# A macaron transformer block on one core: attention taken head pair by head pair over both token halves, output projections moved between the last pairs, and new rules in the planner that orders the instructions

## Chip, cores and metric

The kernel runs on one core of a Trainium2 chip. The metric is the device time of one execution in microseconds (us), lower is better. Engines are named as in the profile: PE (TensorE matmul), PEld (its weight loads), DVE (VectorE), ACT (ScalarE), POOL (GpSimd) and SP (SyncE, which here only issues DMAs).

## What is computed

One layer of a bidirectional encoder over 512 tokens of width 1024, all in float32:

```python
h = h + 0.5 * rms_norm(swiglu(rms_norm(h, ffn1_pre_g), w_gu, w_down), ffn1_post_g)
z = rms_norm(h, mix_pre_g) @ w_in
q_na, k_na, v_na, c_q, c_kv, k_rope = jnp.split(z, split_at, axis=-1)
o_na = neighbourhood_attention(q_na, k_na, v_na, na_rpb)          # 8 heads of 64, 8 x 16 window
o_mla = latent_attention(c_q, c_kv, k_rope, ...)                  # 8 heads, latent q 256, kv 128
mixed = jnp.concatenate([rms_norm(o_na, na_out_norm_g),
                         rms_norm(o_mla, mla_out_norm_g)], axis=-1) @ w_out
h = h + rms_norm(mixed, mix_post_g)
h = h + 0.5 * rms_norm(swiglu(rms_norm(h, ffn2_pre_g), w_gu, w_down), ffn2_post_g)
```

The hidden width of both FFNs is 2816.

## The kernel before, in words

Tokens are held in four tiles of 128 (n = 0 to 3). A float32 product is made of three matmuls on operands split into a high and a low part (`mm3`): high by high, high by low, low by high. Every operand that PE reads in this way must first be cast (ACT, the high part) and subtracted (DVE or POOL, the low part); `split` does both, `load_w` fetches a weight block by DMA and splits it.

The stages in order: FFN1 (`ffn`: first chunks as plain products, the rest in a Winograd form with fewer multiplications), the mixer, FFN2. The mixer runs neighbourhood attention in four head pairs (`na_pair`), the latent compression, the latent attention (`mla_pair(j, hf)`, L1019: head pair j for the token half hf; half 1 holds tokens 2 and 3), and the output projection in two parts. `w_out_a(n, wo)` (L1062) projects the neighbourhood heads of token tile n, two groups of 12 matmuls of 512 columns, one for each half of the output columns. `w_out_b(n, b0, hr)` (L1072) projects the latent heads (24 matmuls), and then runs the token's norms on DVE, ACT and POOL: add, root mean square (`row_rms`: ACT squares with a running sum, DVE scales, POOL raises to the power -1/2), gain, residual, a second norm (FFN2's), and `put_xT`, which transposes the result on PE and splits it for FFN2. In an `mla_pair` a 512-column score tile goes from PE to DVE (row minimum), ACT (exponential), PE (four transposes), ACT and DVE (split), and PE again (product with the values, 256 columns). `put_o` (L773) scales and splits the head outputs and keeps squares for the group's norm, which `o_rstd` (L799) finishes with matmuls of 2 columns.

In the mixer's main sequence (L1089 to L1108) the four pairs of half 1 come first, each with a whole `w_out_a` behind it, then the four pairs of half 0, then `w_out_b` for tokens 2, 3, 0, 1:

```python
for j in range(4):
    mla_pair(j, 1)
    w_out_a((2, 3, 0, 1)[j], wo)
rB = o_rstd(1, (2, 3))
...
for j in range(4):
    mla_pair(j, 0)
```

That order in the code is only the starting point. The class `Plan` (L44) records every instruction with its dependencies (`runs`, `touch`, `add`) and a cost by a small model, places all of them forwards and backwards six times (`place`, `issue`), each time with priorities from the pass before, and at last issues them in the order of the best forward pass. On the chip each engine executes its instructions in that order; an engine whose next instruction waits does nothing behind it. All engine instructions are issued in one line of `issue`, L220 in the profile, so they are told apart by engine, operation and shape.

Of the kernel before, what the change touches and what calls it, by code (L numbers as in the profile page):

```python
# [18 lines left out]
P = 128  # L19
# [24 lines left out]
class Plan:  # L44
# [3 lines left out]
    TAIL = {"ACT": 95, "DVE": 75, "POOL": 60, "PE": 176}  # L48
# [16 lines left out]
    def runs(x):  # L65
# [20 lines left out]
        if kind == "psum":  # L86
            runs = sorted({(a // 512 * 512, (b + 511) // 512 * 512) for a, b in runs})
# [21 lines left out]
    def add(self, eng, op, a, k):  # L109
# [22 lines left out]
        elif eng == "PE":  # L132
            busy = max(109, (cols + 32) / 2.4)
# [15 lines left out]
    def place(self, prio, back):  # L149
# [12 lines left out]
        while done < n:  # L162
            t, e = min((max(free[e], 0.0 if ready[e] else soon[e][0][0]), e) for e in free if ready[e] or soon[e])
            ahead = 0 if e == "PE" or e == "SP" else 250
            while soon[e] and soon[e][0][0] <= t + ahead:
                s, p, i = heappop(soon[e])
                heappush(ready[e], (p, i))
            p, i = heappop(ready[e])
# [5 lines left out]
            if e == "PE" and not back:  # L174
                if s > idle + 1900:
                    warm = s + 3400
                if s < warm:
                    busy *= 2 if busy > 110 else 1.2
                idle = s + busy
            free[e] = s + busy  # L180
            if xfer:
                if back:
                    x = max(s + 500, dma)
                    dma = x + xfer
                    end = dma + 1300 + 330
                else:
                    x = max(s + busy + 1300, dma)
                    dma = x + xfer
                    end = dma + 500
            else:  # L190
                end = s + busy + tail
# [37 lines left out]
def hybrid_block(ctx, tc, A, out):  # L229
# [47 lines left out]
    sqr = cut(512, 1, 2688)  # L277
# [492 lines left out]
    sqs = [h[0][:, 512:], tokt.rearrange("p n c -> p (n c)")]  # L770
    last_sq = [None, None]

    def put_o(j, ps, c0=0):  # L773
# [7 lines left out]
        acc = sqs[g][:, :w]  # L781
        g = j // 4
# [10 lines left out]
        sq = sqr.get()[:, :w]  # L793
        square(sq)
        last_sq[g] = sq
# [3 lines left out]
    def o_rstd(g, ns):  # L799
# [3 lines left out]
        for i, v in enumerate((sqs[g], last_sq[g])):  # L803
            for n in range(len(ns)):
                PE.matmul(b[:, 2 * n : 2 * n + 2], v[:, n * P : (n + 1) * P], ones, start=i + n == 0,
                          stop=i == 1, skip_group_check=True)
# [212 lines left out]
    def mla_pair(j, hf):  # L1019
# [33 lines left out]
        by_column(l, 4, scr[:, 2944:], [r[:, :P], r[:, P:]])  # L1053
# [8 lines left out]
    def w_out_a(n, wo):  # L1062
        t = slice(n * P, (n + 1) * P)
        for hf in range(2):
            c = slice(hf * 512, hf * 512 + 512)
            ps = bank(nb())
            for j in range(4):
                oh, ol = oT[j]
                mm3(ps, (oh[:, t], ol[:, t]), (wo[j][0][:, c], wo[j][1][:, c]), j == 0, j == 3)
            ACT.activation(h[n][:, c], ps, AF.Copy, scale=rA[:, n : n + 1])  # L1070

    def w_out_b(n, b0, hr):  # L1072
# [4 lines left out]
        for j in range(4):  # L1077
            oh, ol = oT[4 + j]
            for hf in range(2):
                c = slice(hf * 512, hf * 512 + 512)  # L1080
                mm3(ps[:, c], (oh[:, t], ol[:, t]), (wo[j][0][:, c], wo[j][1][:, c]), j == 0, j == 3)
        DVE.scalar_tensor_tensor(mx, ps, rB[:, n : n + 1], mx, ALU.mult, ALU.add)
        r = row_rms(mx, ps, 1.0 / 32, EPS, bst)
# [3 lines left out]
        put_xT(n, norm(n, gn, hr, ps, bst), (b0, b0 + 1), mx)  # L1087
# [14 lines left out]
    for j in range(4):  # L1102
# [97 lines left out]
```

## Time and profile before

| what | value |
| --- | --- |
| median of 3 runs | 966.41 us (966.3 to 966.68) |
| the profiled execution | 969.88 us, span 968.1 us |
| mean granted PE clock of the span | 0.991 |
| PE, PEld busy | 948.5 us (98%), 851.8 us (88%) |
| DVE, ACT, POOL busy | 692.8 us (72%), 464.5 us (48%), 302.0 us (31%) |
| DMA | 130.11 MB, mean 134 GB/s |

The profiled execution is 3.47 us above the median. Busy time counts an instruction from start to end; a PE instruction that runs at a lower clock is busy for longer. A row of the view of busy time by stretch has the stretch and its length, then busy time and number of instructions of PE, PEld, DVE, ACT and POOL, then PE's granted clock as a share of full speed (1.00 is 2.4 GHz, 0.50 is 1.2 GHz), the DMA engines' busy share and GB/s. A row of a group by form ends with busy time and mean ns of one instruction, then idle time before them and what ended it. A row in time begins with start and length; the bracket at its end is the idle time of the engine before that row and what ended it. Some matmul records can be missing from a trace.

### The profile page before, as it was taken

The page shows a single profiled execution, that of the slowest core. Times are in us where ns is not written, and L with a number is a line of the kernel's source. Part 1 is how long each engine was busy: PE and PEld are TensorE (multiplying, and loading weights), DVE is VectorE, ACT ScalarE, POOL GpSimd, SP SyncE. Part 2 cuts the span into 40 slices and gives each one's busy share as a digit, 9 for nine tenths or more (in the row PEclk, how much of TensorE's full clock was granted, in tenths as well). Part 3 has the DMA queues.
Part 4 walks back from the last instruction along what each step waited for, and adds up shares of the span by engine and source line. Part 5 has one row for each costly group of instructions (what it writes and reads, how often), then busy time and mean ns, then how long its engine had stood idle before and what let it go on. Part 6 is the DMA issues. An engine that isn't in the chain of part 4 may idle for free. (4 is left out here: it accounts for less than half of the span.)

```text
span 968.1 us, 15209 instructions
## 1 busy us (share of the span) xinstructions
PE 948.5 (98%) x5878; PEld 851.8 (88%) x5878; DVE 692.8 (72%) x963; ACT 464.5 (48%) x801; POOL 302.0 (31%) x240
## 2 busy tenths in 40 slices
PE   9999999999999999999999989899999999999997
PEld 7788999999888888888988878799999999988885
DVE  4896999998522385567686587998999999742224
ACT  5553454444421362677567765764444444441211
POOL 0002767650000013222351422227777574000000
PEclk9999999999999999999999999999999999999999
DMA  9644334359743446122370112454433436753312
GB/s 288 205 156 131 128 132 145 117 155 306 225 113 96 140 159 131 62 75 45 109 165 1 66 44 88 152 183 136 151 120 110 152 127 217 250 170 109 87 44 87
DMA packets 60905, 130.11 MB, mean 134 GB/s; under 512 B 21920, under 2 KB 22816, under 8 KB 60832
## 3 DMA queue, kind: packets, MB, share of 16 engines
q1 hardware_dynamic: 59248, 126.25, 41.6%
q0 software_dynamic: 1008, 1.84, 1.1%
q10 hardware_dynamic: 576, 1.05, 0.3%
q8 instruction: 46, 0.75, 0.3%
q14 instruction: 27, 0.22, 0.1%
HBM read 109.45 MB, written 17.83 MB: 131 GB/s over the span
## 5 line engine op out<-in xcount | busy, mean ns | idle before, releaser
L220 PE MATMUL psum<-memr 128*128 128x256 f32 (+2 forms) x5520 | 921.9, 327 | 7.7 <-ACT memr L220 3.1
L220 PEld LDWEIGHTS psum<-memr 128*128 128x128 f32 x5520 | 809.6, 191 | 94.8 <-DVE memr L220 7.4
L220 DVE TENSOR_TENSOR memr<-m,memr 128x512 fp32r<-128x512 f32 (+3 forms) x310 | 353.7, 1168 | 144.1 <-ACT memr L220 143.9
L220 POOL TENSOR_TENSOR m<-m 128x512 f32<-128x512 f32 (+3 forms) x193 | 264.5, 1385 | 476.0 <-DVE m L220 368.3
L220 ACT CAST memr<-m 128x512 fp32r<-128x512 f32 (+3 forms) x318 | 259.9, 843 | 297.9 <-PE psum L220 213.5
L220 DVE TENSOR_TENSOR m<-psum,m 128x512 f32<-128x512 f32 (+3 forms) x205 | 119.9, 589 | 36.0 <-ACT m L220 21.7
L220 DVE TENSOR_TENSOR memr<-psum,memr 128x512 fp32r<-128x512 f32 (+3 forms) x116 | 68.0, 603 | 30.7 <-ACT memr L220 29.6
L220 ACT CAST memr<-psum 128x512 fp32r<-128x512 f32 (+3 forms) x124 | 62.4, 524 | 41.6 <-PE psum L220 31.8
L220 DVE TENSOR_TENSOR m<-m 128x512 f32<-128x512 f32 (+2 forms) x73 | 72.1, 999 | 6.9 <-ACT m L220 6.0
L220 PE MATMUL psum<-m 128*128 128x128 f32 (+1 forms) x358 | 58.2, 289 | 4.6 <-DVE m L220 2.8
L220 ACT ACTIVATE m<-m 128x512 f32<-128x512 f32 (+3 forms) x78 | 43.9, 564 | 33.1 <-DVE m L220 33.0
L220 PEld LDWEIGHTS psum<-m 128*128 128x128 f32 x358 | 46.6, 162 | 13.8 <-DVE m L220 3.3
L220 ACT COPY m<-psum 128x256 f32<-128x256 f32 (+2 forms) x63 | 26.1, 414 | 46.0 <-PE psum L220 33.9
L220 DVE SCALAR_TENSOR_TENSOR m<-m 128x512 f32<-128x512 f32 (+1 forms) x36 | 33.5, 966 | 4.8 <-POOL m L220 4.3
L220 ACT ACTIVATE m<-psum,m 128x512 f32<-128x512 f32 x40 | 27.4, 688 | 10.9 <-DVE m L220 10.1
L220 POOL MEMSET memr<- 128x256 f32 x8 | 2.5, 312 | 95.9 <-PE psum L220 95.9
L220 ACT ACTIVATE m<-psum 128x512 f32<-128x512 f32 (+2 forms) x27 | 14.0, 519 | 35.8 <-PE psum L220 35.8
L220 ACT ACTIVATE psum<-m 128x1024 f32<-128x1024 f32 x16 | 16.5, 1029 | 16.7 <-DVE m L220 12.1
L220 DVE TENSOR_REDUCE m<-psum 128x1 f32<-128x512 f32 x32 | 21.2, 684 | 1.0 <-PE psum L220 0.7
L220 DVE TENSOR_SCALAR m<-m 128x1 f32<-128x1 f32 (+1 forms) x36 | 6.2, 179 | 21.7 <-ACT m L220 12.2
L220 POOL TENSOR_TENSOR memr<-m,memr 128x1024 fp32r<-128x1024 f32 x8 | 19.3, 2426 | 5.1 <-ACT memr L220 5.1
L220 POOL CAST memr<-memr 64x512 fp32r<-64x512 f32 x8 | 5.8, 730 | 40.6 <-DVE memr L220 40.4
(23 smaller groups left out, 104.8 us busy)
## 6 DMA issues: line engine op xcount, KB each, us to landing
m<-in_ffn_w_gu SPq DMA_DIRECT2D x86, 512.0 KB
m<-in_ffn_w_down SPq DMA_DIRECT2D x44, 512.0 KB
gd<-m SPq DMA_DIRECT2D x44, 256.0 KB
m<-gd SPq DMA_DIRECT2D x44, 256.0 KB
m<-in_x SPq DMA_DIRECT2D x8, 512.0 KB
m<-in_w_qk SPq DMA_DIRECT2D x8, 512.0 KB
h<-m SPq DMA_DIRECT2D x8, 512.0 KB
m<-in_w_out SPq DMA_DIRECT2D x8, 512.0 KB
```

Of the source, the lines that this page charges most:

```text
L220: r = getattr(self.engines[eng], op)(*a, **k)
```

## The change

Two things are changed: the rules by which the planner orders instructions, and the order in which the mixer is written.

Planner: psum dependencies are kept for a whole bank rather than for each half of the partitions; a float32 matmul costs twice; the time from the end of an instruction to the start of one that waits for it on another engine is a number per engine (LAG) in place of 40 ns; SP is held back when DMAs pile up; only longer matmuls keep the modelled clock up; and an engine takes the best ready instruction, or one that becomes ready before that would end if it has a higher priority.

Mixer: the pairs come as (0,1), (0,0), (1,1), (1,0), (2,1), (3,1), each with one or two half projections `w_out_a(n, hf)` of 12 matmuls; then (2,0), `w_out_b(2)`, (3,0), `w_out_b(3)`, `w_out_b(0)`, `w_out_b(1)`. The second set of projection weights gets slots of its own (`w_b`) and is loaded between the pairs. Some scratch tiles move; the squares of `row_rms` in `w_out_b` go to SBUF instead of psum. The number of instructions of each kind stays the same.

```diff
+    ahead, margin = 250, 0
+    TAIL = {"ACT": 95, "DVE": 75, "POOL": 45, "PE": 176}
+    LAG = {"ACT": 60, "DVE": 50, "POOL": 85, "PE": 120, "SP": 60}
...
-            runs = sorted({(a // 512 * 512, (b + 511) // 512 * 512) for a, b in runs})
+            return [((kind, 0), sorted({(a // 512 * 512, (b + 511) // 512 * 512) for a, b in runs}))]
...
-            busy = max(109, (cols + 32) / 2.4)
+            busy = max(109, (cols + 32) / 2.4) * (1 + (op == "matmul" and a[1].dtype == F32))
...
-            ahead = 0 if e == "PE" or e == "SP" else 250
-            while soon[e] and soon[e][0][0] <= t + ahead:
+            while soon[e] and soon[e][0][0] <= t:
...
+            p, i = ready[e][0]
+            if e != "PE" and e != "SP" and soon[e]:
+                c = min(((q, s, j) for s, q, j in soon[e] if s < t + min(ops[i][5], self.ahead)), default=(p, 0, i))
+                if c[0] < p - self.margin:
...
+                    free[e] = max(free[e], dma - 4000) if e == "SP" else free[e]
...
-                est[j] = max(est[j], s + busy if ops[j][0] == e and not xfer else end + 40)
+                same = ops[j][0] == e and not xfer
+                est[j] = max(est[j], s + busy if same else end + (self.LAG[e] + ops[j][6] if back else self.LAG[ops[j][0]]))
...
-        r = row_rms(mx, ps, 1.0 / 32, EPS, bst)
+        sq = reg(Q_AT[6] + 256, 1)
...
+        r = row_rms(mx.rearrange("p (a b c) -> p a b c", a=2, b=2), sq, 1.0 / 32, EPS, bst)
...
-    wo = [load_w(A["w_out"][j], eng=POOL) for j in range(4)]
-    for j in range(4):
-        mla_pair(j, 1)
-        w_out_a((2, 3, 0, 1)[j], wo)
+    wa = [load_w(A["w_out"][j], eng=POOL) for j in range(4)]
+    gp, gn = load_g("mix_post_g"), load_g("ffn2_pre_g")
+    wb = [w_b(0)]
+    parts = [(n, hf) for n in (2, 3, 0, 1) for hf in range(2)]
+    for i, (j, hf) in enumerate(((0, 1), (0, 0), (1, 1), (1, 0), (2, 1), (3, 1))):
+        mla_pair(j, hf)
+        for _ in range((2, 1, 1, 1, 2, 1)[i]):
+            w_out_a(*parts.pop(0))
+        if i == 1:
+            wb.append(w_b(1))
+        if i == 3:
+            wb += [w_b(2), w_b(3)]
     rB = o_rstd(1, (2, 3))
     xb[1] = 26624
-    gp, gn = load_g("mix_post_g"), load_g("ffn2_pre_g")
-    wo = [load_w(A["w_out"][4 + j], eng=POOL) for j in range(4)]
-    for j in range(4):
-        mla_pair(j, 0)
-    for n in (2, 3):
-        w_out_b(n, 5, raws.get())
+    mla_pair(2, 0)
+    w_out_b(2, 5, raws.get())
+    mla_pair(3, 0)
+    w_out_b(3, 5, raws.get())
     o_rstd(1, (0, 1))
-    for n in (0, 1):
-        w_out_b(n, 2 * n, tmps.get())
+    w_out_b(0, 5, tmps.get())
+    w_out_b(1, 0, tmps.get())
```

How the order of the instructions changes, at the three places of which the prediction speaks. The issuing line is L220 before and L233 after. Names: `in_x` are rows of the input, `in_ffn_w_gu` blocks of FFN1's gate and up weights, `m_63` and `memr` the two big SBUF tensors, `gd_68` a DRAM scratch.

SP at the start of the program, before:

```order
L220 DMA m_63<-in_ffn_w_gu 128x1024
L220 DMA m_63<-in_x 128x1x1024 x4
L220 DMA m_63<-in_ident 128x128
L220 DMA m_63<-in_g_o 128x8
L220 DMA m_63<-in_tokt 128x256
L220 DMA m_63<-in_ffn_w_gu 128x1024 x6
L220 DMA gd_68<-m_63 128x512
```

and in the changed kernel:

```order
L233 DMA m_63<-in_ffn_w_gu 128x1024 x2
L233 DMA m_63<-in_x 128x1x1024 x2
L233 DMA m_63<-in_ident 128x128
L233 DMA m_63<-in_x 128x1x1024 x2
L233 DMA m_63<-in_ffn_w_gu 128x1024 x3
L233 DMA m_63<-in_g_o 128x8
L233 DMA m_63<-in_tokt 128x256
L233 DMA m_63<-in_ffn_w_gu 128x1024 x3
```

The second weight block moved ahead of the four rows of the input, and the third to fifth ahead of two small tables.

PE at the start, before (the 128-column matmuls behind the 72 are the first that need rows of the input):

```order
L220 MATMUL psum<-m_63 128x128 x11
L220 MATMUL psum<-memr 128x512 x72
L220 MATMUL psum<-m_63 128x128 x4
L220 MATMUL psum<-memr 128x512 x264
L220 MATMUL psum<-memr 128x256 x1260
```

and in the changed kernel:

```order
L233 MATMUL psum<-m_63 128x128 x11
L233 MATMUL psum<-memr 128x512 x67
L233 MATMUL psum<-m_63 128x128
L233 MATMUL psum<-memr 128x512 x7
L233 MATMUL psum<-m_63 128x128
L233 MATMUL psum<-memr 128x512 x8
L233 MATMUL psum<-m_63 128x128
L233 MATMUL psum<-memr 128x512 x7
L233 MATMUL psum<-m_63 128x128
L233 MATMUL psum<-memr 128x512 x247
L233 MATMUL psum<-memr 128x256 x1260
```

The four products that stood together behind 72 wide matmuls now stand singly, the first behind 67, with 7 or 8 wide ones between them.

PE in the last attention pairs (512 columns: scores and projections; 128: transposes; 256: products with the values), before:

```order
L220 MATMUL psum<-memr 128x256
L220 MATMUL psum<-m_63 128x128 x2
L220 MATMUL psum<-memr 128x256 x7
L220 MATMUL psum<-m_63 128x128 x6
L220 MATMUL psum<-memr 128x512 x6
L220 MATMUL psum<-memr 128x256 x8
L220 MATMUL psum<-m_63 128x128 x4
L220 MATMUL psum<-memr 128x512 x2
L220 MATMUL psum<-m_63 128x128 x4
L220 MATMUL psum<-memr 128x512 x2
L220 MATMUL psum<-m_63 128x128 x4
L220 MATMUL psum<-memr 128x512 x2
```

and in the changed kernel:

```order
L233 MATMUL psum<-memr 128x512 x33
L233 MATMUL psum<-m_63 128x128 x8
L233 MATMUL psum<-memr 128x512 x4
L233 MATMUL psum<-m_63 128x128 x2
L233 MATMUL psum<-memr 128x512 x7
L233 MATMUL psum<-m_63 128x128 x8
L233 MATMUL psum<-memr 128x512 x5
L233 MATMUL psum<-memr 128x256
L233 MATMUL psum<-memr 128x512 x2
L233 MATMUL psum<-m_63 128x128 x4
L233 MATMUL psum<-memr 128x512
L233 MATMUL psum<-memr 128x256 x7
```

The runs of 33, 7 and 5 now hold projections of `w_out_b` among the scores, and the group of 8 at the second row is a token's transposes for FFN2; before, neither stood at this point.

PE at the end of the mixer, before (the three groups of 128 are transposes of the tokens for FFN2, the 256-column matmuls already FFN2's):

```order
L220 MATMUL psum<-memr 128x512 x40
L220 MATMUL psum<-m_63 128x128 x8
L220 MATMUL psum<-memr 128x512 x8
L220 MATMUL psum<-memr 128x256 x28
L220 MATMUL psum<-m_63 128x128 x8
L220 MATMUL psum<-memr 128x256 x10
L220 MATMUL psum<-m_63 128x128 x8
L220 MATMUL psum<-memr 128x256 x154
```

and in the changed kernel:

```order
L233 MATMUL psum<-memr 128x512 x6
L233 MATMUL psum<-memr 128x256 x68
L233 MATMUL psum<-m_63 128x128 x8
L233 MATMUL psum<-memr 128x256 x26
L233 MATMUL psum<-m_63 128x128 x8
L233 MATMUL psum<-memr 128x256 x96
L233 MATMUL psum<-memr 128x512 x48
```

The groups of FFN2 matmuls ahead of the last two groups of transposes grew from 28 and 10 to 68 and 26; the first group of transposes of before now stands earlier, between the attention pairs.

## Rows read from the trace of the kernel before

**Rows 1.** The page: busy time by engine, share of the span.
```profile
PE 948.5 (98%) x5878; PEld 851.8 (88%) x5878; DVE 692.8 (72%) x963; ACT 464.5 (48%) x801; POOL 302.0 (31%) x240
```

**Rows 2.** Busy time by stretch: FFN1; attention pairs with projections between.
```profile
100.00:200.00 100.00, 100.00 (x836) 100.00 (x835) 98.62 (x102) 46.54 (x71) 69.26 (x41) 1.00 0.42 138
485.00:568.00 83.00, 83.00 (x462) 69.73 (x462) 58.92 (x104) 58.58 (x121) 29.13 (x29) 1.00 0.29 74
```

**Rows 3.** PE in time: a run of 512 columns, one of 128.
```profile
484.74 20.51 PE L220 MATMUL psum<-memr 128*128 128x512 f32 x89 [0.21 <-ACT memr L220]
476.61 2.28 PE L220 MATMUL psum<-m 128*128 128x128 f32 x20
```

**Rows 4.** Stretches where PE loses time; small matmuls 476.7 to 484.7.
```profile
23.24:29.96 6.72, 4.79 (x16) 3.24 (x15) 3.98 (x7) 4.12 (x6) 0.55 (x1) 0.75 0.56 184
399.00:476.00 77.00, 76.10 (x456) 67.45 (x457) 52.10 (x171) 54.48 (x149) 21.78 (x34) 1.00 0.24 57
476.61:485.20 8.59, 8.29 (x45) 6.76 (x44) 6.23 (x15) 5.86 (x13) 5.12 (x5) 0.80 0.74 245
568.20:584.00 15.80, 12.54 (x65) 10.33 (x64) 13.19 (x24) 10.55 (x26) 3.72 (x5) 0.78 0.08 33
606.20:620.00 13.80, 9.66 (x65) 8.03 (x64) 12.43 (x15) 8.53 (x16) 4.77 (x4) 1.00 0.54 184
L220 PE MATMUL psum<-m 128*128 128x128 f32 x16 | 3.1, 331 | 0.1
L220 PE MATMUL psum<-m 128*128 128x2 f32 x16 | 1.8, 246 | 0.0
```

**Rows 5.** Busy time by stretch: the three at half clock.
```profile
26.50:29.90 3.40, 3.35 (x7) 2.24 (x8) 3.40 (x5) 2.88 (x4) 0.00 (x0) 0.50 0.39 82
480.46:483.87 3.41, 3.41 (x14) 2.80 (x12) 1.98 (x4) 3.02 (x5) 2.73 (x2) 0.50 0.91 334
576.00:582.90 6.90, 5.97 (x22) 5.18 (x23) 4.80 (x8) 4.04 (x10) 1.52 (x3) 0.51 0.00 0
```

**Rows 6.** Opening in time: PE restart, first and last square, second weight cast.
```profile
26.44 5.74 PE L220 MATMUL psum<-memr 128*128 128x512 f32 x16 [1.44 <-ACT memr L220]
15.42 1.03 ACT L220 ACTIVATE psum<-m 128x1024 f32<-128x1024 f32 x1 [1.26 <-DMA m<-in_x]
22.18 1.03 ACT L220 ACTIVATE psum<-m 128x1024 f32<-128x1024 f32 x1 [1.11 <-DMA m<-in_x]
25.34 1.04 ACT L220 CAST memr<-m 128x1024 fp32r<-128x1024 f32 x1 [2.02 <-DMA m<-in_ffn_w_gu]
```

**Rows 7.** PE by form, 568.2 to 584, and one of its waits in time.
```profile
L220 PE MATMUL psum<-m 128*128 128x128 f32 x28 | 6.0, 345 | 1.7 <-ACT m L220 1.7
L220 PE MATMUL psum<-memr 128*128 128x512 f32 x13 | 5.6, 542 | 0.0
L220 PE MATMUL psum<-memr 128*128 128x256 f32 x24 | 4.5, 316 | 1.6 <-DVE memr L220 0.9 <-ACT memr L220 0.4 <-DVE m L220 0.3
574.47 1.09 PE L220 MATMUL psum<-memr 128*128 128x256 f32 x7 [0.87 <-DVE memr L220]
```

**Rows 8.** PE and DVE by form, 606.2 to 620; POOL's powers in time.
```profile
L220 PE MATMUL psum<-memr 128*128 128x256 f32 x38 | 5.7, 293 | 2.8 <-DVE m L220 1.4 <-ACT m L220 0.7 <-DVE memr L220 0.7
L220 PE MATMUL psum<-m 128*128 128x128 f32 x19 | 2.6, 277 | 1.3 <-DVE m L220 1.3
L220 PE MATMUL psum<-memr 128*128 128x512 f32 x8 | 2.1, 403 | 0.0
L220 DVE SCALAR_TENSOR_TENSOR m<-m 128x1024 f32<-128x1024 f32 x4 | 5.1, 1284 | 1.3 <-POOL m L220 1.3
L220 DVE TENSOR_TENSOR m<-m 128x1024 f32<-128x1024 f32 x2 | 2.4, 1218 | 0.0
603.48 0.54 POOL L220 TENSOR_TENSOR m<-m 128x1 f32<-128x1 f32 x1 [3.75 <-DVE m L220]
605.49 1.45 POOL L220 TENSOR_TENSOR m<-m 128x1 f32<-128x1 f32 x1 [1.46 <-DVE m L220]
```

More of the change, by code (lines that the diff above doesn't have):

```diff
@@ L3 @@
 from contextlib import ExitStack
-from heapq import heappop, heappush
+from heapq import heapify, heappop, heappush
 import numpy as np
@@ L44 @@
 class Plan:
-    TAIL = {"ACT": 95, "DVE": 75, "POOL": 60, "PE": 176}
+    ahead, margin = 250, 0
+    TAIL = {"ACT": 95, "DVE": 75, "POOL": 45, "PE": 176}
+    LAG = {"ACT": 60, "DVE": 50, "POOL": 85, "PE": 120, "SP": 60}
     def __init__(self, tc):
@@ L178, in place @@
                     busy *= 2 if busy > 110 else 1.2
-                idle = s + busy
+                if busy > 115:
+                    idle = s + busy
             free[e] = s + busy
@@ L185, in place @@
                     end = dma + 1300 + 330
+                    free[e] = max(free[e], dma - 4000)
                 else:
@@ L189, in place @@
                     end = dma + 500
+                    free[e] = max(free[e], dma - 4000) if e == "SP" else free[e]
             else:
-                end = s + busy + tail
+                end = s + busy + (0 if back else tail)
             start[i] = s if not back else -(end if xfer else s + busy)
@@ L276, in hybrid_block @@
     tmps = cut(1024, 3)
-    sqr = cut(512, 1, 2688)
+    sqr = scr[:, 2688:3200]
     bst = Ring([new(8) for _ in range(8)])
@@ L769, in hybrid_block @@
     Q_AT = (7168, 5120, 18432, 19456, 20480, 12288, 13312, 25600)
-    sqs = [h[0][:, 512:], tokt.rearrange("p n c -> p (n c)")]
-    last_sq = [None, None]
+    W_AT = ((4096, 4608, 6144, 6656), (7168, 7680, 21504, 22016), (18432, 18944, 22528, 23040), (23552, 24064, 15872, 17920))
+    sqs = [h[0][:, 512:], tts[0][:, :512]]
     def put_o(j, ps, c0=0):
@@ L792, in put_o @@
             return
-        sq = sqr.get()[:, :w]
+        sq = sqr[:, c0 : c0 + w]
         square(sq)
-        last_sq[g] = sq
         if j % 4 < 3:
@@ L802, in o_rstd @@
         w = 2 * len(ns)
-        for i, v in enumerate((sqs[g], last_sq[g])):
-            for n in range(len(ns)):
-                PE.matmul(b[:, 2 * n : 2 * n + 2], v[:, n * P : (n + 1) * P], ones, start=i + n == 0,
+        for i, v in enumerate((sqs[g], sqr)):
+            for n, t in enumerate(ns):
+                PE.matmul(b[:, 2 * n : 2 * n + 2], v[:, t * P : (t + 1) * P], ones, start=i + n == 0,
                           stop=i == 1, skip_group_check=True)
@@ L1052, in mla_pair @@
         r = rowb.get()
-        by_column(l, 4, scr[:, 2944:], [r[:, :P], r[:, P:]])
+        by_column(l, 4, tts[0][:, 512:768], [r[:, :P], r[:, P:]])
         DVE.tensor_tensor(o, r, o, ALU.mult)
@@ L1060, in hybrid_block, with w_out_a, w_b @@
     half, osr = cut(512, 4), cut(256, 2, 2048)
[L1062 to L1066, printed above, removed]
-            for j in range(4):
-                oh, ol = oT[j]
-                mm3(ps, (oh[:, t], ol[:, t]), (wo[j][0][:, c], wo[j][1][:, c]), j == 0, j == 3)
-            ACT.activation(h[n][:, c], ps, AF.Copy, scale=rA[:, n : n + 1])
+    def w_out_a(n, hf):
+        t, c = slice(n * P, (n + 1) * P), slice(hf * 512, hf * 512 + 512)
+        ps = bank(nb())
+        for j in range(4):
+            oh, ol = oT[j]
+            mm3(ps, (oh[:, t], ol[:, t]), (wa[j][0][:, c], wa[j][1][:, c]), j == 0, j == 3)
+        ACT.activation(h[n][:, c], ps, AF.Copy, scale=rA[:, n : n + 1])
+    def w_b(j):
+        to = [reg(o, 512) for o in W_AT[j]]
+        step = [b - a for a, b in zip(W_AT[j][::2], W_AT[j][1::2])]
+        raw = fetch(A["w_out"][4 + j]).rearrange("p (a c) -> p a c", a=2)
+        hi, lo = (bass.AP(tensor=x.tensor, offset=x.offset, ap=[x.ap[0], [d, 2], [1, 512]])
+                  for x, d in zip(to[::2], step))
+        split(hi, lo, raw, POOL)
+        return to[:2], to[2:]
     def w_out_b(n, b0, hr):
@@ L1086, in w_out_b @@
         SP.dma_start(h2[n * P : (n + 1) * P, :], mx)
-        put_xT(n, norm(n, gn, hr, ps, bst), (b0, b0 + 1), mx)
+        r = row_rms(mx.rearrange("p (a b c) -> p a b c", a=2, b=2), sq, 1.0 / 32, EPS, bst)
+        DVE.scalar_tensor_tensor(hr, mx, r, gn, ALU.mult, ALU.mult)
+        put_xT(n, hr, (2, 3), mx)
     for hd in range(1, NH - 1):
```

11 lines of the change are left out of this document (7 added, 4 removed).

## The prediction

> **What bounds the kernel now.** I read the page first, then busy time by stretch, then PE's instructions, then who waits for whom in the stretches that stood out. The profiled execution took 969.88 us for a span of 968.1; the median of the runs shown is 966.41, 3.47 lower. The sums below are made against 969.88 and their difference is taken off the median. A measurement of this kernel can tell about 0.2% (1.9 us) from no change.
>
> PE is busy 98% of the span [rows 1], so the time is PE's work plus what PE loses. To find the loss I need the price of an undisturbed matmul. In FFN1 836 matmuls of 256 columns fill 100 us at full clock [rows 2]: 0.12 us each. A run of 89 of 512 columns takes 20.51 us and 20 of 128 columns 2.28 us [rows 3]: 0.228 and 0.11. With these, any stretch can be priced by its counts and compared with its length:
>
> - 23.24 to 29.96: 16 instructions [rows 4], half of each kind: 8 x 0.228 + 8 x 0.11 = 2.7 of 6.72 us. Lost: 4.0.
> - 399 to 476, neighbourhood attention: the same account leaves some 4 us of the 77, of which PE is idle 0.9 [rows 4].
> - 476.61 to 485.20: 45 instructions, 32 of them of 128 or 2 columns (0.11 us both), so 13 of 512: 32 x 0.11 + 13 x 0.228 = 6.5 of 8.59 us [rows 4]. Lost: 2.1.
> - 485 to 568, latent attention with the first output projections between its pairs: loses nothing that I can price; PE is busy 83.00 of 83 us at full clock, DVE 58.92 [rows 2].
> - 568.20 to 584, the last pairs with no projection left between them: 28 x 0.11 + 13 x 0.228 + 24 x 0.12 = 8.9 of 15.8 us [rows 7]. Lost: 6.9.
> - 606.20 to 620, the last norms: 19 x 0.11 + 38 x 0.12 + 8 x 0.228 = 8.5 of 13.8 us [rows 8]. Lost: 5.3.
>
> After 620 FFN2 runs like the stretch of [rows 2]. So some 22 us are to be had, in five places.
>
> A part of this is not idle time. In three stretches the clock is at 0.50 or 0.51 of full speed, the 1.2 GHz level, while PE works: 3.40, 3.41 and 6.90 us [rows 5]; half of that, 1.7, 1.7 and 3.4 us, is lost while PE counts as busy. The first and the last follow waits of PE of 1.44 and 1.38 us; before the middle one PE was hardly idle and issued transposes and 2-column matmuls. The Trainium skill (Perfetto Trace Analysis, Identifying the Most-Contended Engine) says the same in general: the matmul busy share is no good measure of headroom, since matmuls are pipelined; weight-load busy time is better. Here that is 88% against 98% [rows 1]. By busy time the change could return the idle alone, which is the second rival below.
>
> **The change, part by part.** Instruction counts are the same, so only losses move. The edits to the planner's cost rules (LAG, TAIL, whole psum banks, doubled cost of fp32 matmuls, queue backlog, lookahead) have one price together: that of the order which comes out.
>
> *Opening.* SP now issues the second block of FFN1's weights ahead of the four x rows. Before, it stood behind them: the x rows reach ACT from 15.42 to 22.18, one each 2.25 us, and the block only at 25.34 [rows 6], and PE stands 1.44 us for its cast, then runs at half clock. Moved past four x rows it lands about 4 x 2.25 = 9 us earlier, near 16, and each x row about 2.25 later, the last near 24.5. The four small diagonal products that need the x rows are now put one by one among 22 matmuls of 512 columns, 5 us of cover (67 x 0.228 from 8 us on reaches 23.3 before the first). Who is late next: the last x row's chain, whose square takes 1.03 us from 24.5 on [rows 6], a reciprocal root behind it, ahead of the last product near 28.5. I take all 4.0 us. Bounds: 0 (another block late instead) to 4.0.
>
> *Neighbourhood attention.* The same pairs in a slightly different interleaving. Of the 4 us I take 1.0; bounds -1 to 2.5.
>
> *Latent compression (476 to 485).* 2-column products now come mixed with the transposes and the 512-wide matmuls, and the first token's transposes later after the last matmul they wait for. Of 2.1 I take 1.2; bounds 0 (half clock stays) to 2.1.
>
> *Pairs.* The eight half projections of the attention group, 96 matmuls or 21.9 us of cover, were used up by the first four pairs. They now stand behind six pairs, and the output projections of tokens 2 and 3, 24 matmuls or 5.5 us each, stand beside the last two pairs instead of behind them. So every pair has cover as between 485 and 568. What is put past what: the long DVE chain of these two tokens' norms (1.28 and 1.22 us each [rows 8]) now stands in DVE's queue between the pairs' reductions and splits, which PE waits for. In a window of some 24 us I count 21 to 23 us of DVE work, so DVE has little left, and I charge 0.6 us. The second set of projection weights is split on POOL earlier than before, none of it near the end. Together 6.9 + 0.7 (the slightly lossy stretch behind it) - 0.6 = 7.0. Bounds: 2 (DVE late at half of the places) to 7.6.
>
> *Last norms.* Tokens 0 and 1 are last in both. Before, 28 and 10 matmuls of FFN2 stand ahead of the last two groups of transposes (38 x 0.12 = 4.6 us), now 68 and 26 (11.3 us). That would cover all of the 5.3. But the two tokens' chains, which begin one well behind the other before, now begin 1.6 us apart by my walk through the order, and share DVE: each has three 1.28 us steps and one of 1.22, and a 1.22 us split of what it transposes. Along the chain PE stands about 2.6 us before the last transposes and 1.7 in three shorter waits, 4.3. Gain 1.0; less 0.7 for a stretch at half clock of 3.4 us (1.7 lost) at a chance of 40%. So 0.3; bounds -2 to 3.
>
> In this chain the step on POOL depends on its neighbour on DVE. The 128x1 power took 0.54 us alone and 1.45 us when it began beside a 1.22 us DVE operation with two SBUF inputs [rows 8]. The Trainium skill (SBUF - State Buffer, Who interferes with whom) has it that such an operation contends with a GpSimd instruction that reads SBUF, over a shared port pair. By it, each of the four powers of tokens 0 and 1 could cost 0.9 more or less with the new order, 3.6 us at most. My walk puts the long value on two of the four, as the trace of before has them.
>
> Sum: 4.0 + 1.0 + 1.2 + 7.0 + 0.3 = 13.5. The profiled execution would come out at 956.4, the median at 966.41 - 13.5 = **952.9**.
>
> **The rivals.**
>
> 1. *The opening's gain is given back.* The x rows come 2.25 us later, so do the normalisation factors and all that DVE does for FFN1's first chunks; DVE is busy 98.62 of 100 us there [rows 2]. If PE catches up with DVE, the 4.0 us become a wait in FFN1. For it: DVE has next to no spare time. Against: PE is busy all 100.00 us of that stretch, so DVE is ahead of it everywhere now, and by more than the 4 + 2.25 us by which the two come closer as far as I can follow the operands of each matmul. Time: 952.9 + 4.0 = 956.9.
>
> 2. *Only idle time returns.* The half clock comes back wherever some wait is left: 1.7 + 1.7 + 3.4 = 6.8 us. For it: one of the three stretches has no wait before it. Against: the others do, and their waits go. Time: 959.7.
>
> 3. *Slower: DVE's queue blocks the pairs.* The place is the last four pairs. DVE executes in order; with a 1.28 us norm step in front, a reduction or split is late, and PE stands as at 574.47 (0.87 us for DVE [rows 7]), then runs at half clock: 6.9 us a time. Two such places and the gain is gone (952.9 + 13.8 = 966.7); from three on it is slower: 952.9 + 20.7 = 973.6. For it: DVE is busy 13.19 of 15.8 us in that stretch [rows 4]. Against: from 485 to 568 DVE has 71% with weight splits and pairs side by side and PE never stands.
>
> 4. *No change.* The five gains are separate and small; if only the last norms and attention move, the time stays within 1.9 us of 966.4. For it: PE at 98%. Against: the opening's order alone moves a landing by 9 us.
>
> **How the numbers follow.** Forecast 0.62, rival 1 0.14, rival 2 0.16, rival 3 0.04, rival 4 0.04. Forecast and the first two are faster; no change takes rival 4 less a part that ends faster: 0.93 faster, 0.03 same, 0.04 slower. Low end: all upper bounds would give 966.41 - (4.0 + 2.5 + 2.1 + 7.6 + 3) = 947.2, and not all hold; 948.5. High end: rival 2 holds, 960.
>
> **What would show it.** Right: the second weight block's cast near 16 us and no half clock at 26 us; PE busy throughout the last pairs at full clock; DVE some 85% busy there; a remaining gap of 2 to 3 us before the last transposes near 610. Wrong: an idle PE within FFN1 behind DVE (rival 1), stretches at 0.50 of the clock in the same places (rival 2), PE waiting for DVE between the last pairs (rival 3).

## The result, and the profile after

The changed kernel takes 956.50 us (median of 4 runs, 956.17 to 959.28) against 966.36 before (4 runs, 965.72 to 966.68): a ratio of 0.9899, 95% interval 0.9876 to 0.9922. That is 9.9 us faster. The forecast was 13.5 us, 952.9; the range of 948.5 to 960.0 holds the result. On another chip before ran at 967.42 (11 runs) and the changed kernel at 956.80 (5 runs), a ratio of 0.9890 (0.9872 to 0.9908). The experiments below ran on three chips, on which before took 967.65, 967.42 and 966.80.

The page of the profile after: the span, busy time by engine (to be held against [rows 1]) and the group of PE's wide matmuls, with the same group of the page before under it.

```profile
span 954.8 us, 15205 instructions
...
PE 939.8 (98%) x5878; PEld 847.8 (89%) x5878; DVE 693.6 (73%) x963; ACT 462.7 (48%) x801; POOL 304.8 (32%) x240
...
L233 PE MATMUL psum<-memr 128*128 128x256 f32 (+2 forms) x5520 | 917.0, 326 | 2.5 <-ACT memr L233 1.5
...
L220 PE MATMUL psum<-memr 128*128 128x256 f32 (+2 forms) x5520 | 921.9, 327 | 7.7 <-ACT memr L220 3.1
```

PE is busy 8.7 us less for the same 5878 instructions, and the wide matmuls wait 2.5 us in all instead of 7.7. Stretches of the profile after that answer to [rows 2] and [rows 4] (columns as there):

```profile
23.24:29.96 6.72, 6.72 (x35) 5.62 (x34) 2.30 (x6) 3.59 (x6) 1.34 (x3) 1.00 0.73 244
30.00:350.00 320.00, 320.00 (x2011) 291.04 (x2010) 236.01 (x270) 136.61 (x192) 96.72 (x63) 1.00 0.51 160
100.00:200.00 100.00, 100.00 (x835) 100.00 (x835) 92.75 (x101) 47.28 (x71) 72.42 (x41) 1.00 0.41 133
472.00:481.00 9.00, 8.06 (x49) 6.27 (x48) 7.64 (x16) 6.19 (x13) 7.55 (x6) 1.00 0.34 117
481.00:564.00 83.00, 83.00 (x471) 70.18 (x470) 64.53 (x115) 63.87 (x133) 28.38 (x30) 1.00 0.32 80
564.00:606.00 42.00, 41.28 (x258) 35.86 (x256) 33.78 (x48) 23.85 (x46) 11.56 (x13) 1.00 0.35 126
598.00:616.00 18.00, 14.64 (x118) 13.83 (x118) 15.79 (x22) 10.50 (x19) 4.27 (x4) 1.00 0.31 110
```

The window of 23.24 to 29.96, which held 16 PE instructions, now holds 35 at full clock. The attention pairs and the stretch behind them (481 to 606) have PE busy 124.28 of 125 us at full clock; before, 568 to 584 alone lost 6.9. In FFN1 PE never waits from 30 to 350 us; DVE, which was busy 98.62 of the 100 us from 100 to 200, is busy 92.75. Up to PE's last matmul there is no stretch at half clock in this execution.

The second weight block's cast and the last input row's square on ACT, then PE in time at the opening and at the end of the mixer:

```profile
16.85 1.05 ACT L233 CAST memr<-m 128x1024 fp32r<-128x1024 f32 x1 [1.17 <-DMA m<-in_ffn_w_gu]
...
26.19 1.03 ACT L233 ACTIVATE psum<-m 128x1024 f32<-128x1024 f32 x1 [0.90 <-DMA m<-in_x]
```

```profile
8.55 2.23 PE L233 MATMUL psum<-memr 128*128 128x512 f32 x7 [0.63 <-ACT memr L233]
11.02 12.56 PE L233 MATMUL psum<-memr 128*128 128x512 f32 x54 [0.24 <-DVE memr L233]
...
398.98 0.44 PE L233 MATMUL psum<-m 128*128 128x128 f32 x2 [1.09 <-ACT m L233]
...
611.79 1.06 PE L233 MATMUL psum<-m 128*128 128x128 f32 x8 [2.50 <-DVE m L233]
```

What is left: the opening begins with two waits for the transposed input, 0.63 and 0.24 us; the first transposes of neighbourhood attention wait 1.09 us for ACT, which loads a table for 1.28 us ahead of the exponential (nothing was tried on that); the compression stage still stands for 0.94 of 9 us; and the last transposes wait 2.50 us for DVE, where the prediction had 2.6.

The 969.88 of the profile before and the 956.59 of the one after differ by 13.3 us, the forecast's 13.5 almost exactly. The medians differ by 9.9. Where the other 3.4 us are is what the first experiment asks.

### The profile page after: what moved, and what is told of

Same layout as the page of the kernel before. It is cut to its first block, busy times and chain, and to the rows that moved or that the text cites. A ratio compares the mean times of both kernels' runs of the same rounds, so it can differ in the third digit from the quotient of the medians.

```text
span 954.8 us, 15205 instructions
## 1 busy us (share of the span) xinstructions
PE 939.8 (98%) x5878; PEld 847.8 (89%) x5878; DVE 693.6 (73%) x963; ACT 462.7 (48%) x801; POOL 304.8 (32%) x240
## 5 line engine op out<-in xcount | busy, mean ns | idle before, releaser
L233 PE MATMUL psum<-memr 128*128 128x256 f32 (+2 forms) x5520 | 917.0, 326 | 2.5 <-ACT memr L233 1.5
L233 PEld LDWEIGHTS psum<-memr 128*128 128x128 f32 x5520 | 807.1, 190 | 86.0 <-ACT memr L233 4.9
L233 DVE TENSOR_TENSOR memr<-m,memr 128x512 fp32r<-128x512 f32 (+3 forms) x310 | 348.7, 1150 | 135.9 <-ACT memr L233 135.7
L233 POOL TENSOR_TENSOR m<-m 128x512 f32<-128x512 f32 (+4 forms) x193 | 267.8, 1402 | 465.1 <-DVE m L233 320.6
L233 ACT CAST memr<-m 128x512 fp32r<-128x512 f32 (+3 forms) x318 | 260.7, 843 | 284.1 <-PE psum L233 202.7
L233 DVE TENSOR_TENSOR m<-psum,m 128x512 f32<-128x512 f32 (+3 forms) x205 | 120.2, 589 | 43.5 <-ACT m L233 21.5
L233 DVE TENSOR_TENSOR memr<-psum,memr 128x512 fp32r<-128x512 f32 (+3 forms) x116 | 67.5, 602 | 22.8 <-ACT memr L233 21.6
L233 ACT CAST memr<-psum 128x512 fp32r<-128x512 f32 (+3 forms) x124 | 62.1, 523 | 40.2 <-PE psum L233 31.5
L233 DVE TENSOR_TENSOR m<-m 128x512 f32<-128x512 f32 (+2 forms) x73 | 77.2, 1064 | 5.5 <-ACT m L233 5.2
L233 PE MATMUL psum<-m 128*128 128x128 f32 (+1 forms) x358 | 56.5, 279 | 5.3 <-DVE m L233 3.9
L233 ACT ACTIVATE m<-m 128x512 f32<-128x512 f32 (+3 forms) x78 | 44.0, 566 | 30.8 <-DVE m L233 29.9
L233 PEld LDWEIGHTS psum<-m 128*128 128x128 f32 x358 | 46.3, 157 | 13.3 <-ACT memr L233 2.7
L233 ACT COPY m<-psum 128x256 f32<-128x256 f32 (+2 forms) x63 | 25.9, 416 | 49.9 <-PE psum L233 43.7
L233 DVE SCALAR_TENSOR_TENSOR m<-m 128x512 f32<-128x512 f32 (+1 forms) x36 | 33.8, 965 | 4.9 <-POOL m L233 4.3
L233 POOL MEMSET memr<- 128x256 f32 x8 | 2.5, 312 | 96.3 <-PE psum L233 96.3
L233 ACT ACTIVATE m<-psum,m 128x512 f32<-128x512 f32 x40 | 27.0, 687 | 10.7 <-DVE m L233 7.8
L233 ACT ACTIVATE m<-psum 128x512 f32<-128x512 f32 (+2 forms) x27 | 13.9, 518 | 36.8 <-PE psum L233 36.8
L233 ACT ACTIVATE memr<-m 128x512 fp32r<-128x512 f32 (+2 forms) x28 | 20.8, 758 | 14.3 <-DVE m L233 11.6
L233 POOL TENSOR_TENSOR memr<-m,memr 128x1024 fp32r<-128x1024 f32 x8 | 19.1, 2392 | 15.0 <-ACT memr L233 13.4
L233 POOL CAST memr<-memr 64x512 fp32r<-64x512 f32 x8 | 5.4, 674 | 52.2 <-DVE memr L233 52.2
L233 DVE TENSOR_REDUCE m<-psum 128x1 f32<-128x512 f32 x32 | 21.2, 681 | 0.1
L233 DVE TENSOR_SCALAR m<-m 128x1 f32<-128x1 f32 (+1 forms) x36 | 6.3, 179 | 19.7 <-ACT m L233 11.1
```

Source lines behind the costliest of these rows:

```text
L233: r = getattr(self.engines[eng], op)(*a, **k)
```

## The experiments

The theory after the result: the change removes waits in the places that the prediction names, and the profiled execution of before held more time at half clock than its other executions, so that a sum made against it promises too much. There are two rivals. The half clock may belong to the order of the instructions; or the changed kernel may lose again, elsewhere and in other runs, what its profile shows as gained.

### The kernel before, profiled again

No edit.

> The kernel before, unchanged, profiled once more. Theory (the profiled execution of before held half-clock stretches that its other runs mostly lack): the median stays at 966.4 within 0.5 us, the mean granted clock of most runs is above the 0.991 of the profile, and the new profile shows fewer than the three half-clock stretches [rows 5] and a span 2 to 4 us below 968.1. Rival (the half clock belongs to this order of instructions, the profiler costs the 3.5 us): all runs at 0.991, the same three stretches again.

Measured: 967.58 us (12 runs, 964.78 to 968.85), ratio 1.0 (0.9988 to 1.0011). The median was expected within 0.5 us of 966.4 and lies 1.2 above it, on another chip. The profiled execution took 964.78, the fastest of the twelve, with a span of 963.0, which is 5.1 us shorter where 2 to 4 were expected, and a mean granted clock of 0.996. Stretches of it at the places of the half clock of [rows 5], and one behind them:

```profile
24.00:28.00 4.00, 2.81 (x15) 2.02 (x14) 2.70 (x5) 3.23 (x6) 0.55 (x1) 1.00 0.43 165
478.00:482.00 4.00, 3.66 (x18) 2.07 (x16) 2.65 (x8) 3.76 (x6) 2.82 (x2) 1.00 0.94 317
574.46:580.50 6.04, 6.04 (x43) 5.37 (x44) 5.71 (x10) 5.23 (x12) 0.59 (x2) 1.00 0.07 7
606.00:610.00 4.00, 3.18 (x15) 3.18 (x16) 3.57 (x5) 1.80 (x5) 2.36 (x2) 0.58 0.41 135
```

At 24 and at 478 the clock is full, and also right behind 574.46, where the same wait ends as at 576.93 before. Instead there is one stretch at half clock, from 606.6. PE in time in this execution:

```profile
27.02 5.29 PE L220 MATMUL psum<-memr 128*128 128x512 f32 x22 [0.53 <-DVE memr L220]
...
606.82 4.55 PE L220 MATMUL psum<-memr 128*128 128x256 f32 x24 [1.37 <-DVE m L220]
```

and in the first profile of before:

```profile
576.93 1.12 PE L220 MATMUL psum<-m 128*128 128x128 f32 x4 [1.38 <-ACT m L220]
...
611.89 3.13 PE L220 MATMUL psum<-memr 128*128 128x256 f32 x24 [1.37 <-DVE m L220]
```

The wait of 1.37 us and the 24 matmuls at 606.82 are those of 611.89 before; there they took 3.13 us, here 4.55, at half clock. At the opening the waits themselves differ: 1.44 us with a fall behind it in the first profile, 0.53 and no fall here. So the same program loses clock in different places in different executions, here for 3.4 us at a time, which costs 1.7 where PE has work throughout. At the two waits of the mixer the clock differs though the wait is the same. To compare kernels I summed one minus the granted clock over windows of 1 us, up to PE's last matmul, and call the time less this loss the rest:

| profiled execution | time | lost at half clock | the rest |
| --- | --- | --- | --- |
| before, first profile | 969.88 | 6.8 | 963.1 |
| before, second profile | 964.78 | 1.7 | 963.1 |
| after, first profile | 956.59 | 0.0 | 956.6 |
| after, second profile | 956.74 | 1.7 | 955.0 |

The rest is the same for both profiles of before, so the 5.1 us between them are clock. The theory holds for before and the first rival falls: the median run, at 966.4 to 967.6, comes out at two or three such stretches, where the first profile held four (three falls, one of them of double length). The change takes 6.5 to 8.1 us off the rest; the remainder of its 9.9, 1.8 to 3.4 us, is then less time at half clock in the median run. The second rival falls with the runs on the other chip, where the changed kernel is 10.6 us faster again. The two profiles of the changed kernel differ by 1.6 us in the rest, 1.1 of it at the opening (see below).

### The planner's rules alone, and the mixer's order alone

The first kernel has the changed class `Plan` and the mixer of before; the second the old `Plan` and the new mixer. The edit of the first, in short:

```diff
-class Plan:  (before)
+class Plan:  (changed)
...
     for j in range(4):
         mla_pair(j, 1)
         w_out_a((2, 3, 0, 1)[j], wo)
```

> The planner's new rules alone, mixer written as before. Theory (gains lie in places and add up): the opening and attention/compression gains come from the rules, 2.8 + 2.6 us in the profiles, so about 961.5. Rival (the rules matter only with the new mixer order): 965 to 967.

> The mixer's new order alone, planned by the old rules. Theory: the pairs' gain of 5.9 us and some of the end's 1.8 come from having projections between all pairs, whatever the rules: 959 to 961. Rival (the old rules cannot place the norms between the last pairs, DVE's queue blocks them): 963 or more, with PE waits for DVE between the last pairs.

Measured, against 967.65 for before (17 runs): the rules alone 961.31, ratio 0.9941 (0.9924 to 0.9957); the mixer alone 963.25, ratio 0.9954 (0.9940 to 0.9967). 6.3 and 4.4 us add to 10.7, near the 10.6 of the whole change on the other chip. The rest, as in the table, is 958.0 and 960.1.

The rules alone keep the old mixer's waits, in the view by stretch (the last pairs) and in PE's rows there:

```profile
560.00:582.00 22.00, 19.90 (x126) 16.06 (x125) 20.79 (x38) 18.85 (x44) 6.85 (x9) 1.00 0.24 80
```

```profile
562.94 0.39 PE L233 MATMUL psum<-memr 128*128 128x256 f32 x1 [0.42 <-ACT memr L233]
...
568.73 1.10 PE L233 MATMUL psum<-memr 128*128 128x256 f32 x7 [0.65 <-DVE memr L233]
```

PE waits at the same steps as in [rows 7], among them 0.42 us for ACT and 0.65 us for DVE. So the new rules do not fill these waits where no projection is left to fill them; that part of the gain is the mixer's. The mixer alone fills them under the old rules too (PE is busy 82.84 of 83 us and 37.67 of 38), and loses at the end:

```profile
485.00:568.00 83.00, 82.84 (x468) 68.42 (x467) 63.71 (x112) 62.96 (x131) 28.52 (x30) 1.00 0.34 85
568.00:606.00 38.00, 37.67 (x227) 31.95 (x226) 30.57 (x45) 21.50 (x44) 9.31 (x11) 1.00 0.37 125
606.00:622.00 16.00, 12.77 (x92) 12.16 (x91) 13.97 (x19) 10.04 (x18) 2.81 (x3) 0.89 0.24 97
```

```profile
616.01 1.06 PE L220 MATMUL psum<-m 128*128 128x128 f32 x8 [2.58 <-DVE m L220]
```

The wait before the last transposes, 2.58 us, is there with the old rules as well as with the new: it belongs to the new mixer. (With the old mixer the new rules leave other waits at the end, 2.20 us before a product and 0.96 before the last transposes.) With it and the half clock behind it (0.89 of the clock from 606 to 622) the mixer alone stayed 2 us short of its expectation (959 to 961). Its time is in the range of the rival (963 or more), but the rival's sign, waits between the last pairs, is not there. The expectation took 5.9 us for the pairs from the first two profiles, and 3.4 us of that are half clock of the first [rows 5]. The rules came out as expected.

### The opening alone, and taken back

Each of the two kernels has its first 185 instructions in the order of the other kernel; all others keep theirs.

```diff
-        for i in sorted(range(n), key=lambda i: (best[1][i], i)):
+        order = sorted(range(n), key=lambda i: (best[1][i], i))
+        first = set(OPENING)
+        for i in OPENING + [i for i in order if i not in first]:
```

> The kernel before with the first 185 instructions (to about 29 us) in the changed kernel's order, nothing else. Theory: 2 to 3 us less, 963.5 to 964.5, second weight cast near 17 us, no PE wait at 25 us. Rival (the later input rows make DVE late in FFN1 and give it back): 966.4, with PE waits between 30 and 350 us.

> The changed kernel with the first 185 instructions (to about 31 us) in the order of before. Theory (the opening is a part of its own, worth about 3.9 us as in the opening experiment): 3 to 4.5 us above the changed kernel, 960 to 961.5. Rival (the opening's gain needs the old mixer, or is eaten elsewhere in the changed kernel): within 1 us of the changed kernel.

Measured: before with the new opening 963.74, ratio 0.9964 (0.9950 to 0.9978), 3.9 us faster. The changed kernel with the old opening 961.41 against 956.80, 4.6 us slower. The opening is a part of its own and nothing of it is given back in FFN1. The weight casts and the last row's square on ACT, and FFN1 from 30 to 350 us, in the kernel before with the new opening:

```profile
13.06 1.05 ACT L234 CAST memr<-m 128x1024 fp32r<-128x1024 f32 x1 [0.47 <-DMA m<-in_ffn_w_gu]
14.86 1.05 ACT L234 CAST memr<-m 128x1024 fp32r<-128x1024 f32 x1 [0.74 <-DMA m<-in_ffn_w_gu]
...
23.90 1.03 ACT L234 ACTIVATE psum<-m 128x1024 f32<-128x1024 f32 x1 [1.03 <-DMA m<-in_x]
```

```profile
30.00:350.00 320.00, 319.94 (x2007) 290.70 (x2008) 240.59 (x268) 133.60 (x191) 93.25 (x63) 1.00 0.51 160
```

The second block is cast at 14.86 and not at 25.34, and the last input row's square starts at 23.90 and not at 22.18; PE is busy 319.94 of 320 us. Of the 3.9 us, 1.5 are waits (963.1 to 961.6 of the rest). The others are clock, as far as the means tell: the median granted clock of the runs is 0.996 with the new opening and 0.994 for before. Of the four profiles with the old opening, two show waits of 1.44 and 1.08 us for a weight cast near 26 us and a fall of the clock behind them, and two (before again and the mixer alone) waits of 0.53 and 0.52 us for DVE and no fall. Whether the early block or the products put singly bring the gain was not tried apart.

### A wait at the end that the change itself brought in

In the profile after, token 0's chain and token 1's chain stand on DVE and ACT like this:

```profile
596.37 1.06 ACT L233 ACTIVATE memr<-m 128x1024 fp32r<-128x1024 f32 x1 [1.85 <-DVE m L233]
...
601.68 1.06 ACT L233 ACTIVATE memr<-m 128x1024 fp32r<-128x1024 f32 x1 [3.21 <-DVE m L233]
...
602.86 1.06 ACT L233 ACTIVATE memr<-m 128x1024 fp32r<-128x1024 f32 x1
```

```profile
595.06 1.28 DVE L233 SCALAR_TENSOR_TENSOR m<-psum,m 128x1024 f32<-128x1024 f32 x1 [1.40 <-PE psum L233]
...
597.39 1.28 DVE L233 SCALAR_TENSOR_TENSOR m<-psum,m 128x1024 f32<-128x1024 f32 x1
```

Token 1's sum is ready at 598.67 (the second of the sums from psum, from 597.39), but its square starts at 602.86, right behind token 0's second square at 601.68; ACT stands 3.21 us before that one. Both write the same scratch tile: the change moved the squares of `row_rms` in `w_out_b` out of psum into one SBUF tile for all tokens, and so the planner has to keep them in the order of the code.

```diff
         sq = r_(bass.AP(tensor=sq.tensor, ...))
+        if n == 1:
+            sq = ps.rearrange("p (a b c) -> p a b c", a=2, b=2)
```

> The changed kernel, but token 1's squares go to its own psum banks (as before the change) and not to the SBUF scratch shared by all tokens. Theory (the shared scratch makes token 1's first square wait for token 0's second, ACT idle 3.2 us beside it): the wait before the last transposes falls from 2.5 us to under 1, the time 1.5 to 2.5 us below the changed kernel. Rival (DVE, which runs both tokens' chains, sets the end): the wait stays above 2 us, the time within 0.5 us.

> The changed kernel, unchanged, on the chip of the other runs. Theory (fewer waits of PE, so fewer half-clock stretches): 956.5 to 958; most runs have none or one stretch (clock 0.996 to 0.999) where before has two or three (0.992 to 0.995); the wait of 2.5 us before the last transposes is there again. Rival (the change only hit a lucky profile): clock as before, 959 or more.

Measured on the same chip: the changed kernel 956.80 (955.49 to 957.88), with token 1's own scratch **953.34** (952.90 to 955.11), ratio to before 0.9858 (0.9838 to 0.9878). A second time it took 954.01 (952.61 to 955.21), ratio 0.9867 (0.9846 to 0.9889).

> The version with a scratch of its own for token 1, once more. Theory: 952.5 to 954.5 again, mean granted clock 0.998 or more in most runs. Rival (the first look was lucky): 956 or more.

ACT and PE of this version at the end of the mixer:

```profile
595.91 1.06 ACT L233 ACTIVATE memr<-m 128x1024 fp32r<-128x1024 f32 x1 [1.87 <-DVE m L233]
...
597.22 1.03 ACT L233 ACTIVATE psum<-m 128x1024 f32<-128x1024 f32 x1 [0.16 <-DVE m L233]
...
600.20 1.06 ACT L233 ACTIVATE memr<-m 128x1024 fp32r<-128x1024 f32 x1 [0.89 <-DVE m L233]
```

```profile
604.28 1.09 PE L233 MATMUL psum<-m 128*128 128x128 f32 x8 [0.51 <-DVE m L233]
...
608.23 0.63 PE L233 MATMUL psum<-m 128*128 128x128 f32 x4
...
608.92 0.60 PE L233 MATMUL psum<-m 128*128 128x128 f32 x4
```

Token 1's first square starts at 597.22, ahead of token 0's second at 600.20, and the last transposes wait for nothing. The wait was the shared scratch's, not DVE's load. The gain is 3.5 us for a wait of 2.5, above the 1.5 to 2.5 expected: with the wait, the changed kernel ran at 0.994 to 0.998 of the clock (median 0.996), without it at 0.998 or 0.999 in four of five runs. In the second set two of four ran at 0.994, with a stretch of half clock at 475 in the profile, so that the expectation on the clock held in half of the runs only.

### All squares back in psum

```diff
-        sq = reg(Q_AT[6] + 256, 1)
-        sq = r_(bass.AP(tensor=sq.tensor, ...))
+        sq = ps.rearrange("p (a b c) -> p a b c", a=2, b=2)
```

> The changed kernel with the squares of all four tokens in the token's own psum banks, as before the change. Theory (only token 1's wait for the shared scratch costs anything): as the version with token 1 alone, 952.5 to 954.5, wait before the last transposes under 1 us. Rival (the scratch was moved out of psum because the banks are needed: the next token's products then wait for the squares): 1 us or more above that version, PE waits at the projections of tokens 3 and 0.

Measured: 957.72 us, ratio 0.9904 (0.9886 to 0.9922), 3.7 us above the second measurement of the version with token 1 alone, on the same chip. The rival holds. PE in time:

```profile
575.10 4.14 PE L233 MATMUL psum<-memr 128*128 128x512 f32 x10 [2.09 <-ACT psum L233]
```

The projections of token 3 wait 2.09 us for ACT's square of token 2 to leave psum, bank 5, which three of the four tokens share. Here the move to SBUF pays; for token 1, with banks 0 and 1, it only cost. Which of the other two tokens need it was not tried.

### Where the projections are written, and how many there are

```diff
     mla_pair(2, 0)
-    w_out_b(2, 5, raws.get())
     mla_pair(3, 0)
+    w_out_b(2, 5, raws.get())
     w_out_b(3, 5, raws.get())
```

> The changed kernel with the output projections of tokens 2 and 3 written behind both last pairs instead of between them. Theory (the planner places by readiness, the written order matters only through shared buffers): within 1 us of the changed kernel, no new PE waits between the pairs. Rival (where they are written decides): 3 us or more above it, with waits as at 574 to 577 in before.

Measured: 956.31 (4 runs) against 956.80. The time is the same, as the theory has it, and PE is busy 124.16 of the 125 us from 481 to 606 (124.28 in the profile after): the planner takes these projections as filler wherever they are ready.

```diff
-        for _ in range((2, 1, 1, 1, 2, 1)[i]):
+        for _ in range((2, 1, 1, 0, 0, 0)[i]):
```

> The changed kernel with only the first four of the eight half projections computed; tokens 0 and 1 get no projection of the neighbourhood heads, 48 matmuls of 512 columns (48 x 0.228 = 10.9 us of PE) are left out, so the pairs (1,0), (2,1) and (3,1) have no projection behind them. Theory (the projections are cover, PE waits for DVE and ACT without them): the time falls by much less than 10.9 us below the changed kernel's 956.8, to 948 to 953, with PE waits in those pairs. Rival (the new order of the pairs is what removed the waits, the projections are only work): it falls by the full 10.9, to 946 or less.

This kernel leaves out half of the neighbourhood heads' projection. Measured: 948.53 us, 8.3 below the changed kernel for 10.9 us of work left out (7.7 against before of the same chip). PE in time:

```profile
499.13 1.10 PE L233 MATMUL psum<-memr 128*128 128x256 f32 x7 [0.50 <-DVE memr L233]
...
582.91 0.96 PE L233 MATMUL psum<-memr 128*128 128x512 f32 x3 [1.20 <-ACT memr L233]
```

Waits of 0.50 and 1.20 us are back among the pairs, and one stretch of half clock behind the second. By stretches:

```profile
481.00:553.00 72.00, 71.30 (x413) 59.34 (x412) 58.91 (x107) 58.54 (x123) 28.58 (x29) 1.00 0.47 97
553.00:595.00 42.00, 40.22 (x236) 34.14 (x235) 33.97 (x50) 25.08 (x49) 12.55 (x13) 0.96 0.38 123
```

PE is idle 0.70 and 1.78 us here, and 0.72 in all from 481 to 606 in the profile after. That the projections are cover holds; how much they cover is small, 10.9 - 8.3 = 2.6 us (3.2 against before of the same chip) for half of them, the half clock among it. The cover of the last two pairs, the projections of tokens 2 and 3, was not taken away by itself.

## Why the prediction was right, and where not

**The five places** were the right ones. Against the first profile, by when PE reaches the same instruction:

- *Opening, 4.0 us.* The first FFN1 matmul of 256 columns starts 2.8 us earlier (88.23 to 85.43). The wait and its half clock went as forecast, the second block's cast came at 16.85 for "near 16", but the last input row at 26.19 for "near 24.5". 1.3 us were lost ahead of that place: the first of the four diagonal products starts at 23.41, five wide matmuls (1.1 us) earlier in the order than before, where it started at 23.24. These are mostly the waits of 0.63 and 0.24 us for the transposed input, which landed later in this execution (ACT's second cast of it starts at 7.77, before at 6.53); the profile of the kernel before with the new opening has its first product at 22.18, and in the second profile of the changed kernel the first matmul of 256 columns starts at 84.31, 3.9 us earlier than before. In the medians the opening alone gave 3.9.
- *Neighbourhood attention, 1.0.* Mis-sized: from there to the last matmul of 416 columns another 2.4 us were gained (476.42 to 471.19, less the 2.8). It was the term with the least working behind it. The gain belongs to the new rules: this stretch takes 386.0 us with the rules alone, and 388.1 with the mixer alone, as in before (388.2).
- *Compression, pairs and end, 1.2 + 7.0 + 0.3 = 8.5.* Measured 8.1 to the end of PE's work (960.84 to 947.52, less the 5.2). By idle time and half clock, compression fell from 2.0 to 0.9 us (1.1 for the 1.2), the pairs with what follows them from 6.8 to 0.7 (6.0 for the 7.0), and the end from 4.1 to 3.4 (0.8, where 1.0 less 0.7 for half clock was taken). DVE is busy 78% and 80% of the two stretches from 481 to 606, not 85%; PE is idle 0.72 us there for the 0.6 taken. The end has its wait of 2.50 for the 2.6 that I walked along the chain, and the half clock behind it came in some executions. The row of before for the pairs and what follows:

```profile
568.20:606.00 37.80, 34.44 (x182) 28.55 (x181) 28.59 (x49) 22.79 (x50) 9.39 (x13) 0.91 0.21 70
```

The parts sum to 13.3 of 13.5. That is in part luck: the opening's 1.2 too little in this execution and attention's 1.4 too much cancel. **The step that failed** is the last of the sum: "The sums below are made against 969.88 and their difference is taken off the median." The 13.5 contained all 6.8 us of half clock of that one execution, three of the stretches in [rows 5], and the median run of before does not have them all: it is 3.47 us, two stretches of 1.7, below the profile. Taken off, 13.3 - 3.5 = 9.8, and 9.9 was measured. This needs the profile after to stand for its median run, which it does (956.59 and 956.50), again by luck: it lost nothing at half clock, but some 1.1 us at the opening. The number stood in the first paragraph of the prediction and its reason was not asked.

**The rivals.** The opening's gain was not given back (first rival: PE busy 320.00 of 320 us from 30 to 350), though the time measured, 956.5, is nearest to the 956.9 of that rival; the time alone would have pointed to the wrong cause. The second expected 6.8 us of half clock to stay in the changed kernel. It went, but the median run of before had only about half of it to lose, so the time came out between forecast and rival. The Trainium skill's sentence there (Perfetto Trace Analysis, Identifying the Most-Contended Engine) agrees with the two pages: PE's busy share is 98% before and after, for a span that is 13.3 us shorter. DVE's queue did not block the pairs (third), and the time moved far beyond 0.2% (fourth).

**A right number for a wrong reason.** The 2.6 us before the last transposes were put down to two chains that share DVE. DVE had room: with a scratch of its own for token 1 the wait is gone. What held it was a dependency that the edit on the scratch brought in, and which the prediction put at nothing. The powers on POOL in time after, with the DVE step behind the third:

```profile
598.81 1.46 POOL L233 TENSOR_TENSOR m<-m 128x1 f32<-128x1 f32 x1 [4.05 <-DVE m L233]
603.10 0.55 POOL L233 TENSOR_TENSOR m<-m 128x1 f32<-128x1 f32 x1 [2.83 <-DVE m L233]
605.17 1.40 POOL L233 TENSOR_TENSOR m<-m 128x1 f32<-128x1 f32 x1 [1.53 <-DVE m L233]
609.46 0.86 POOL L233 TENSOR_TENSOR m<-m 128x1 f32<-128x1 f32 x1 [2.89 <-DVE m L233]
...
606.60 1.28 DVE L233 SCALAR_TENSOR_TENSOR m<-m 128x1024 f32<-128x1024 f32 x1 [0.44 <-POOL m L233]
```

and before, behind those of [rows 8]:

```profile
610.79 2.65 POOL L220 TENSOR_TENSOR m<-m 128x1 f32<-128x1 f32 x2 [3.85 <-DVE m L220]
616.33 1.39 POOL L220 TENSOR_TENSOR m<-m 128x1 f32<-128x1 f32 x1 [2.89 <-DVE m L220]
```

The long ones, 1.46 and 1.40 us, began beside DVE's 1.22 us multiplication by the gain, the 0.86 beside one of 0.68, the 0.55 alone: two of four, as taken. The Trainium skill (SBUF - State Buffer, Who interferes with whom) agrees with that. The trace of before did not have two of four, as the prediction says: with 605.49 of [rows 8], all four powers of tokens 0 and 1 were long there, 1.22 to 1.45 us. Nor is 0.9 us the price of a long one: DVE multiplies for most of that time, and its next step stands 0.44 us behind the power. What made the wait of 2.5 was the scratch.

## What to carry to other kernels

Before a sum is made against a profiled execution, ask what in it is not in the other runs: here its distance to the median was about two stretches at half clock. A stall that is filled gains its own length and, where a clock drop tends to follow it, more in some runs, so count the two apart. When a scratch tile is merged for several users, look for the order that it forces on them: giving one token of four its own made the fastest version that does all the work, 953.3 us.

## What was not expected of the hardware

PE's clock does not fall in the same places in every execution of a kernel. Thirteen executions were profiled; up to PE's last matmul, eleven of them hold 15 falls, each of about 3.4 us at 0.50, three of double that. 11 begin in a wait of PE of about 1 us or more, or within about 2 us of its end, and 4 in the compression stage (475 to 481 us), with its transposes and 2-column matmuls. But such a wait need not bring one. The profile after has a wait of 2.50 us with full clock behind it, while its second profile, with the same wait of 2.48, runs at half clock from 612.3. The wait of 1.06 to 1.09 us ahead of the first attention transposes stands in nine of the profiles, with full clock behind it in all. What decides it is not shown.

The runs of one kernel thus spread: the 51 of before over 6 us (963.5 to 969.8). Time times mean granted clock spreads less, 959.7 to 963.4, with the clock on record to three digits (0.001 is 1 us). It does not explain all: the first four runs of the changed kernel give 951.6 to 955.6 by it, for times of 956.2 to 959.3.
